# A filler step between logits and transposes, and row scales behind the next block, in a two-layer retention and differential-attention trunk

## The chip, the core and the metric

The kernel runs on one core of a Trainium2 chip. The metric is the device time of one execution in microseconds (us), taken as the median of several runs. Behind the times stands a profile of one execution: every instruction of the five engines with its start and duration, the DMA transfers, and the clock that was granted to TensorE. In the profile PE is TensorE, DVE is VectorE, ACT is ScalarE, POOL is GpSimd and SP is SyncE, which only issues DMAs.

## The reference

Two layers over 1024 tokens of width 1024, float32. Layer 0 is a retention mixer, layer 1 differential attention with 16 heads; each has an input projection with a SiLU gate, an output projection and RMS norms around it. The change lies in layer 1:

```python
def block(args):                       # 128 queries against all keys, per head
    qblk, start = args
    logits = jnp.einsum('bhmqd,bhmkd->bhmqk', qblk, k)    # m: two maps per head, d = 64
    logits = jnp.where(mask, logits + bias[None, :, None], -jnp.inf)
    probs = jax.nn.softmax(logits, axis=-1)
    attn = probs[:, :, 0] - lam * probs[:, :, 1]
    return jnp.einsum('bhqk,bhke->bhqe', attn, v)

out = lax.map(block, (qb, starts))
out = rmsnorm(out, subln_g, eps=GN_EPS) * (1.0 - lambda_init)   # per head and query
gated = jax.nn.silu(g) * out
return gated @ w_out
```

## The kernel before

Products are made at nearly float32 precision from pairs of fp32r parts, high and low: each product of two operands is three matmuls (high x high, high x low, low x high). Layer 1 is `attention_layer`. Its main loop runs over 16 heads and, in each, over 8 blocks of 128 queries in the order 6, 2, 3, 7, 4, 0, 1, 5 (`ORDER`); block i sees the keys of blocks 0 to i. One turn of the loop, a step, does this:

- `logits` of the next block (lines 760 to 767): full-width products for the high parts (L760), then narrow ones over 64 rows of the array for the low parts (L767), or, for blocks 0 and 1, products with a query padded with zeros (L763). They go to two PSUM tiles "S", one for each of the two maps.
- `attn_t` of the present block (L821): up to four transposes of the probabilities e, by TensorE, into the one PSUM bank "T"; ScalarE copies them out as `ath` (L824) and VectorE makes `atl` (L825). Blocks 4 to 7 have a second group of transposes later in the step.
- `softmax` of the next block, on VectorE and ScalarE: maxima (L792, L794), negation (L795), exponentials that read S (L797), then reciprocal and combination of the two maps into e (L800, L801, L803).
- `square_sum` of the last finished pair of blocks (L857, L858: products with ones), its copy `ssr` (L860) and a DMA to DRAM (`ssd`).
- after each odd block, `values` (L835 to L837) for a pair of blocks, with the squares (L843 to L845).

TensorE's order is written out by hand: instructions stand in it as the program issues them. The other engines' order is set by the scheduler of the framework. Between these pieces TensorE is given filler: a generator, `filler_gen`, that yields steps of three 512-wide products (lines 215 to 217, and 616 to 618 for the gates; or three 256-wide ones, 658 to 660), all projections of later heads, and at its end the first products of the output projection (lines 122 to 124 in `out_mm`). `pull` takes one step and adds its estimated cost to a clock `clk`; `fill_until(t)` pulls until that clock reaches t; `fill_total` keeps the supply at a steady pace at the end of each step. `ready` is the clock time from which the transposes of the next block may be issued; it is counted from the logits by `SLACK["base"]` and `SLACK["wide"]`. When the supply is empty `pull` does nothing.

Heads are gathered in three batches, 0 to 7, 8 to 11 and 12 to 15. At the end of a batch the square sum of its last pair is made at once, and in the next step `row_scales` loads all square sums of the batch (`rss`), transposes the softmax sums in bank "T" (L869), copies them to `rsr` (L872) and makes the row scales (L873, L874 and the reciprocal root). Pieces of the gated output are then scaled one per step by `finish`. The last batch's row scales come behind the loop.

Of the kernel before, what the change touches and what calls it, by code (L numbers as in the profile page):

```python
# [50 lines left out]
class _Trunk:  # L51
# [525 lines left out]
    def attention_layer(self, HR, QR, pmm, ws0, slots):  # L577
        nc, io = self.nc, self.io
        with ExitStack() as es:
# [308 lines left out]
            for _ in v_proj(0):  # L888
                pass
            pend = None  # L890
            rows = None
            todo = []
            ready = 0.0
            ready_o = 0.0
# [1 line left out]
            for s, (h, i) in enumerate(seq):  # L896
# [4 lines left out]
                if nxt is not None:  # L901
                    if nxt[0] not in bts:
                        load_bias(nxt[0])
                    need("qk", nxt[0])
                    if s % TB == 2:
                        narrow_q(h)
                    need("qk", seq[min(s + AHEAD, len(seq) - 1)][0])
                    fill_until(ready - SLACK["qk"])
                    Ss = logits(*nxt)
                    nready = clk["pe"] + SLACK["base"] + SLACK["wide"] * (nxt[1] + 1) / 8.0  # L910
                fill_until(ready)
                attn_t(h, i, A, 0)
                t_done = clk["pe"]
                if rows is not None:
                    row_scales(*rows)
                    todo += [None] * 8 + [(tb, h0) for h0 in range(*BATCHES[rows[0]], 4) for tb in range(TB)] + [()]
                    rows = None
                elif todo:
                    step = todo.pop(0)
                    if step:  # L920
                        finish(*step)
                    elif step == ():
                        finish_store()
# [7 lines left out]
                if pend is not None:  # L931
                    fill_until(ready_o)
                    square_sum(*pend)
                    pend = None
                if i % 2 == 1:
                    need("v", h // 2)
                    if h < LATE:
                        need("g", h)
                    fill_until(t_done + SLACK["av"])
                    pend = (h, i // 2) + values(h, i // 2)  # L940
                    ready_o = clk["pe"] + SLACK["sq"]
                    if i == ORDER[-1] and h + 1 in (BATCHES[0][1], BATCHES[1][1]):
                        fill_until(ready_o)
                        square_sum(*pend)
                        pend = None
                        rows = (batch(h)[0],)
                n_ = s + 1
                if RATE * n_ / 8.0 <= total:
                    fill_total(RATE * n_ / 8.0)
# [144 lines left out]
```

## Time and profile before

| | us |
|---|---|
| median of three runs | 2177.19 |
| lowest, highest | 2174.77, 2178.92 |
| the profiled execution | 2180.56 |
| span of its instructions | 2178.6 |
| attention loop in the span | about 922 to 2005 |

The profiled execution is 2 us longer than its span, from the first to the last instruction. Layer 0 fills the span up to 922 us, the attention loop follows, and from 2005 us the output projection of layer 1. In the timeline each row has the start in us from the span's start, the duration, the engine, the line, the operation, what is written and read, shapes and the number of instructions that are merged (x4), and in brackets the idle time of the engine ahead of it and what ended that. TensorE's instructions overlap: a 512-wide product lasts 0.4 us, but the next one starts 0.235 us behind it.

### The profile page before, as it was taken

How to read it: one execution, taken by the hardware profiler on the slowest of the kernel's cores; microseconds unless marked ns; L12 is line 12 of the kernel's file. 1: busy time of each engine (PE TensorE's matmuls, PEld its weight loads, DVE VectorE, ACT ScalarE, POOL GpSimd, SP SyncE). 2: the span in 40 equal slices, each digit the busy share in tenths (PEclk: the TensorE clock that was granted, in tenths of full speed). 3: DMA queues.
4: the chain of work that ended last, by engine and by line, in shares of the span. 5: the costliest groups of instructions: out<-in, count | busy, mean ns of one | idle time of the engine just before them, and what ended most of it. 6: DMA issues, size and time to landing. Idle time of an engine off the chain costs nothing.

```text
span 2178.6 us, 31078 instructions
## 1 busy us (share of the span) xinstructions
PE 2130.3 (98%) x11861; PEld 1793.9 (82%) x11861; DVE 1293.9 (59%) x3188; ACT 851.5 (39%) x1638; POOL 427.4 (20%) x246
## 2 busy tenths in 40 slices
PE   7999999999999999999999999999999999999998
PEld 7888988898897788787888888888787878877876
DVE  6254344434437438736777667777777777776644
ACT  4121221122123333335555455554545555544321
POOL 2332501511512000121111111111133111211300
PEclk9999999999999999999999999999999999999999
DMA  4112112111212544311111111111244113334743
GB/s 164 65 39 68 57 39 73 47 54 54 63 55 98 176 158 166 121 49 42 40 46 42 40 49 42 39 37 43 85 136 134 47 38 95 115 101 146 256 152 133
DMA packets 98916, 185.48 MB, mean 85 GB/s; under 512 B 8848, under 2 KB 51024, under 8 KB 98640
## 3 DMA queue, kind: packets, MB, share of 16 engines
q1 hardware_dynamic: 63824, 166.50, 23.5%
q10 hardware_dynamic: 34944, 17.01, 2.6%
q8 instruction: 93, 1.52, 0.3%
q14 instruction: 55, 0.45, 0.1%
HBM read 147.67 MB, written 38.95 MB: 86 GB/s over the span
## 4 chain that ended last, share of the span: by engine, by line
PE 89%; DVE 4%; DMA 3%; issue 2%; ACT 1%; SPq 0%; POOL 0%; DVEq 0%; ACTq 0%; POOLq 0%
PE ps_mm L158 6%; PE ps_mm L157 6%; PE ps_mm L159 5%; PE ps_mm L215 5%; PE ps_mm L216 5%; PE ps_mm L217 5%; PE ps_mm L122 4%; PE ps_mm L123 4%; PE ps_mm L124 4%; PE ps_t L821 3%; PE ps_ret L398 3%; PE ps_s L760 3%; PE ps_mm L658 3%; PE ps_mm L167 3%; PE ps_mm L169 3%; PE ps_mm L168 3%
## 5 line engine op out<-in xcount | busy, mean ns | idle before, releaser
L83 POOL TENSOR_TENSOR w_l<-w_raw,w_h 128x1024 fp32r<-128x1024 f32 x112 | 271.6, 2431 | 1169.3 <-ACT w_h L82 1137.6
L797 ACT ACTIVATE e<-ps_s,nm 128x896 f32<-128x896 f32 (+7 forms) x256 | 189.8, 742 | 111.3 <-DVE nm L795 101.9
L215 PE MATMUL ps_mm<-RB,w_h 128*128 128x512 f32 x512 | 209.8, 410 | 0.4 <-ACT RB L150 0.4
L157 PE MATMUL ps_mm<-RA,w_h 128*128 128x512 f32 x512 | 204.6, 400 | 1.2 <-DVE sg L428 1.1
L158 PE MATMUL ps_mm<-RA,w_h 128*128 128x512 f32 x512 | 205.4, 401 | 0.0
L216 PE MATMUL ps_mm<-RB,w_h 128*128 128x512 f32 x512 | 202.9, 396 | 1.5 <-DVE RB L151 1.5
L217 PE MATMUL ps_mm<-RB,w_l 128*128 128x512 f32 x512 | 202.7, 396 | 0.0
L159 PE MATMUL ps_mm<-RA,w_l 128*128 128x512 f32 x512 | 202.4, 396 | 0.0
L824 ACT CAST ath<-ps_t 128x512 fp32r<-128x512 f32 (+1 forms) x192 | 91.9, 478 | 221.4 <-PE ps_t L821 205.5
L82 ACT CAST w_h<-w_raw 128x1024 fp32r<-128x1024 f32 x112 | 117.5, 1049 | 123.5 <-PE ps_mm L158 38.8
L792 DVE TENSOR_REDUCE mx<-ps_s 128x1 f32<-128x640 f32 (+2 forms) x192 | 119.4, 622 | 76.7 <-PE ps_s L767 72.5
L111 DVE TENSOR_TENSOR g_l<-w_raw,g_h 128x1024 fp32r<-128x1024 f32 x60 | 84.1, 1402 | 107.4 <-ACT g_h L110 107.3
L658 PE MATMUL ps_mm<-w_h,RB 128*128 128x256 f32 x512 | 147.3, 288 | 0.0
L169 PE MATMUL ps_mm<-w_h,RA 128*128 128x256 f32 x512 | 145.6, 285 | 0.0
L167 PE MATMUL ps_mm<-w_h,RA 128*128 128x256 f32 x512 | 144.9, 285 | 0.6 <-ACT RA L150 0.6
L168 PE MATMUL ps_mm<-w_l,RA 128*128 128x256 f32 x512 | 144.8, 284 | 0.1
L660 PE MATMUL ps_mm<-w_h,RB 128*128 128x256 f32 x512 | 143.5, 280 | 0.0
L659 PE MATMUL ps_mm<-w_l,RB 128*128 128x256 f32 x512 | 143.5, 280 | 0.0
L110 ACT CAST g_h<-w_raw 128x1024 fp32r<-128x1024 f32 x60 | 62.9, 1049 | 167.9 <-PE ps_mm L123 125.5
L157 PEld LDWEIGHTS ps_mm<-RA,w_h 128*128 128x128 f32 x512 | 96.4, 188 | 24.7 <-DVE sg L428 1.6
L217 PEld LDWEIGHTS ps_mm<-RB,w_l 128*128 128x128 f32 x512 | 96.5, 189 | 23.7
L159 PEld LDWEIGHTS ps_mm<-RA,w_l 128*128 128x128 f32 x512 | 96.6, 189 | 22.4
(216 smaller groups left out, 5408.4 us busy)
## 6 DMA issues: line engine op xcount, KB each, us to landing
w_raw<-in_wn SPq DMA_DIRECT2D x64, 512.0 KB
w_raw<-in_wv SPq DMA_DIRECT2D x32, 512.0 KB
w_raw<-in_wo SPq DMA_DIRECT2D x32, 512.0 KB
w_raw<-g SPq DMA_DIRECT2D x32, 512.0 KB
w_raw<-g1f SPq DMA_DIRECT2D x24, 512.0 KB
xt<-in_x SPq DMA_DIRECT2D x16, 512.0 KB
w_raw<-in_wg SPq DMA_DIRECT2D x16, 512.0 KB
g<-go ACTq DMA_DIRECT2D x32, 256.0 KB
```

What stands on the lines that cost most here:

```text
L83: nc.gpsimd.tensor_sub(l, raw, _f32(h))
L157: nc.tensor.matmul(ps, wh[:, k], region[:, kt, cols], start=(kt == 0), stop=False)
L158: nc.tensor.matmul(ps, wh[:, k], region[:, 8 + kt, cols], start=False, stop=False)
L159: nc.tensor.matmul(ps, wl[:, k], region[:, kt, cols], start=False, stop=(kt == KT - 1))
L167: nc.tensor.matmul(ps, region[:, kt, cols], wh[:, k], start=(kt == 0), stop=False)
L168: nc.tensor.matmul(ps, region[:, kt, cols], wl[:, k], start=False, stop=False)
L169: nc.tensor.matmul(ps, region[:, 8 + kt, cols], wh[:, k], start=False, stop=(kt == KT - 1))
L215: nc.tensor.matmul(ps, wh[:, k], HR[:, kt, tok], start=(kt == 0), stop=False)
L216: nc.tensor.matmul(ps, wh[:, k], HR[:, 8 + kt, tok], start=False, stop=False)
L217: nc.tensor.matmul(ps, wl[:, k], HR[:, kt, tok], start=False, stop=(kt == KT - 1))
L658: nc.tensor.matmul(ps[:, t, :], HR[:, kt, cols], wh[:, k], start=(kt == 0), stop=False)
L797: nc.scalar.activation(e[:, 0:n], S[:, 0:n], AF.Exp, bias=nm, accum_out=(s0 if m == 0 else s1))
```

## The change

One filler step is pulled right behind the logits, and `ready` is counted from behind it. `row_scales` moves ahead of the transposes of its step. At the end of a batch the square sum is no longer made at once, but, as all others, in the following step, behind that step's transposes; the row scales then come one step later than before.

```diff
--- before.py
+++ after.py
@@ -888,7 +888,7 @@
             for _ in v_proj(0):
                 pass
             pend = None
-            rows = None
+            rows = closing = None
             todo = []
             ready = 0.0
             ready_o = 0.0
@@ -907,12 +907,14 @@
                     need("qk", seq[min(s + AHEAD, len(seq) - 1)][0])
                     fill_until(ready - SLACK["qk"])
                     Ss = logits(*nxt)
+                    pull()
                     nready = clk["pe"] + SLACK["base"] + SLACK["wide"] * (nxt[1] + 1) / 8.0
+                if rows is not None:
+                    row_scales(*rows)
                 fill_until(ready)
                 attn_t(h, i, A, 0)
                 t_done = clk["pe"]
                 if rows is not None:
-                    row_scales(*rows)
                     todo += [None] * 8 + [(tb, h0) for h0 in range(*BATCHES[rows[0]], 4) for tb in range(TB)] + [()]
                     rows = None
                 elif todo:
@@ -932,6 +934,8 @@
                     fill_until(ready_o)
                     square_sum(*pend)
                     pend = None
+                    if closing is not None:
+                        rows, closing = (closing,), None
                 if i % 2 == 1:
                     need("v", h // 2)
                     if h < LATE:
@@ -939,11 +943,8 @@
                     fill_until(t_done + SLACK["av"])
                     pend = (h, i // 2) + values(h, i // 2)
                     ready_o = clk["pe"] + SLACK["sq"]
-                    if i == ORDER[-1] and h + 1 in (BATCHES[0][1], BATCHES[1][1]):
-                        fill_until(ready_o)
-                        square_sum(*pend)
-                        pend = None
-                        rows = (batch(h)[0],)
+                    if i == ORDER[-1] and h + 1 in [h1 for h0, h1 in BATCHES[:-1]]:
+                        closing = batch(h)[0]
                 n_ = s + 1
                 if RATE * n_ / 8.0 <= total:
                     fill_total(RATE * n_ / 8.0)
```

How this moves instructions is seen on TensorE. In an ordinary step of head 0 (the logits of block 2 in L760 and L767, then the first transposes of block 6):

```order
 L760 MATMUL ps_s<-RA 128x384 x2
 L767 MATMUL ps_s<-RA 128x384 x2
+L215 MATMUL ps_mm<-RB,w_h 128x512
+L216 MATMUL ps_mm<-RB,w_h 128x512
+L217 MATMUL ps_mm<-RB,w_l 128x512
 L821 MATMUL ps_t<-ident,e 128x128 x4
 L215 MATMUL ps_mm<-RB,w_h 128x512
```

The three products of a filler step stand between the narrow products and the transposes; the same supply has one step less further on.

The end of the first batch on TensorE, before: the square sum of head 7 (L857, L858), the logits of head 8, the transposes of its first block, the row-scale transpose L869, and filler.

```order
L857 MATMUL ps_o<-sqh,ones 128x256
L858 MATMUL ps_o<-sql,ones 128x256
L760 MATMUL ps_s<-RA 128x384 x2
L767 MATMUL ps_s<-RA 128x384 x2
L821 MATMUL ps_t<-ident,e 128x128 x4
L869 MATMUL ps_t<-ident,s0all 64x128
L616 MATMUL ps_mm<-RB,w_h 128x512
L617 MATMUL ps_mm<-RB,w_h 128x512
```

Now: the end of the transposes of head 8's first block, the square sum of head 7, and, after four filler steps that are left out, the logits of the next block, one filler step, L869 and the transposes.

```order
L821 MATMUL ps_t<-ident,e 128x128 x3
L857 MATMUL ps_o<-sqh,ones 128x256
L858 MATMUL ps_o<-sql,ones 128x256
...
L760 MATMUL ps_s<-RA 128x512 x2
L767 MATMUL ps_s<-RA 128x512 x2
L616 MATMUL ps_mm<-RB,w_h 128x512
L617 MATMUL ps_mm<-RB,w_h 128x512
L618 MATMUL ps_mm<-RB,w_l 128x512
L869 MATMUL ps_t<-ident,s0all 64x128
L821 MATMUL ps_t<-ident,e 128x128 x3
L616 MATMUL ps_mm<-RB,w_h 128x512
```

L869 stands ahead of the transposes that use the same bank and one step later, and the square sum behind transposes.

The last block of the last head on TensorE, before: its logits (L760, L767), the transposes of the block ahead of it (x2), filler, its own transposes (x4, x2) and the square sum. The first gap holds eight more filler steps and six value products, the second two filler steps.

```order
L760 MATMUL ps_s<-RA 128x384 x4
L767 MATMUL ps_s<-RA 128x384 x4
L821 MATMUL ps_t<-ident,e 128x128 x2
L122 MATMUL ps_mm<-RA,g_h 128x512
L123 MATMUL ps_mm<-RA,g_h 128x512
L124 MATMUL ps_mm<-RA,g_l 128x512
...
L821 MATMUL ps_t<-ident,e 128x128 x4
...
L821 MATMUL ps_t<-ident,e 128x128 x2
L857 MATMUL ps_o<-sqh,ones 128x256
```

Behind these logits 11 filler steps stand ahead of the last transposes. Now:

```order
L760 MATMUL ps_s<-RA 128x384 x4
L767 MATMUL ps_s<-RA 128x384 x4
L821 MATMUL ps_t<-ident,e 128x128 x2
L835 MATMUL ps_o<-ath,RA 128x256
L836 MATMUL ps_o<-atl,RA 128x256
L837 MATMUL ps_o<-ath,RA 128x256
...
L821 MATMUL ps_t<-ident,e 128x128 x6
L857 MATMUL ps_o<-sqh,ones 128x256
L858 MATMUL ps_o<-sql,ones 128x256
L835 MATMUL ps_o<-ath,RA 128x256
```

No filler is left behind these logits; the six transposes stand in one row, and the gap holds value products only (L837 among them). On VectorE, in the same place, before: the combination of the block ahead (L803, 256 wide), then the first maximum of the last block, and the copy of the transposes.

```order
L803 SCALAR_TENSOR_TENSOR e<-e,arr 128x256
L792 TENSOR_REDUCE mx<-ps_s 128x1
L794 ISA ps_s,mx<-ps_s,bt,mx 128x256
L794 ISA mx 128x1
L825 TENSOR_TENSOR atl<-ps_t,ath 128x2x128
L795 TENSOR_SCALAR nm<-mx 128x1
```

The maximum follows the combination at once. Now the low part of a gated tile (L111, for the output projection) stands between them.

```order
L803 SCALAR_TENSOR_TENSOR e<-e,arr 128x256
L111 TENSOR_TENSOR g_l<-w_raw,g_h 128x1024
L792 TENSOR_REDUCE mx<-ps_s 128x1
L825 TENSOR_TENSOR atl<-ps_t,ath 128x2x128
L794 ISA ps_s,mx<-ps_s,bt,mx 128x256
```

L111 has moved ahead of the last block's first maximum; before it stood behind that block's second negation.

## Rows read from the trace of the kernel before

**Rows 1.** The page: its head, and part 1, busy time, share of the span and instructions.

```profile
span 2178.6 us, 31078 instructions
...
PE 2130.3 (98%) x11861; PEld 1793.9 (82%) x11861; DVE 1293.9 (59%) x3188; ACT 851.5 (39%) x1638; POOL 427.4 (20%) x246
```

**Rows 2.** Who waited for whom, TensorE, 922 to 1990 us: total, times, longest.

```profile
PE ps_t L821 <- DVE atl L825: 4.6, 4, 2.0
PE ps_t L821 <- DVE e L803: 4.0, 5, 1.8
PE ps_s L760 <- ACT e L797: 3.3, 3, 1.2
PE ps_t L869 <- DVE atl L825: 2.8, 2, 1.4
PE ps_o L836 <- DVE atl L825: 2.3, 1, 2.3
PE ps_o L836 <- DVE nm L795: 1.9, 3, 0.8
```

**Rows 3.** Timeline of TensorE (start, us, work), a block's transposes right behind narrow products.

```profile
1240.28 0.73 PE L767 MATMUL ps_s<-RA 64*128 64x512 f32 x4
1240.94 0.66 PE L821 MATMUL ps_t<-ident,e 128*128 128x128 f32 x4
```

**Rows 4.** Timeline of TensorE, a filler step right behind narrow products.

```profile
1693.15 0.50 PE L215 MATMUL ps_mm<-RB,w_h 128*128 128x512 f32 x1
1693.48 0.40 PE L216 MATMUL ps_mm<-RB,w_h 128*128 128x512 f32 x1
1693.72 0.39 PE L217 MATMUL ps_mm<-RB,w_l 128*128 128x512 f32 x1
```

**Rows 5.** Timeline of TensorE, transposes behind a filler, and behind padded-query products.

```profile
1970.79 0.60 PE L821 MATMUL ps_t<-ident,e 128*128 128x128 f32 x4
...
1976.80 0.62 PE L821 MATMUL ps_t<-ident,e 128*128 128x128 f32 x4
```

**Rows 6.** Timeline of TensorE, the longest wait for the probabilities.

```profile
1641.76 0.63 PE L821 MATMUL ps_t<-ident,e 128*128 128x128 f32 x4 [1.83 <-DVE e L803]
```

**Rows 7.** Timeline of all engines, end of the first batch of heads; idle time in brackets.

```profile
1487.80 0.30 PE L869 MATMUL ps_t<-ident,s0all 128*64 128x128 f32 x1 [1.40 <-DVE atl L825]
...
1491.41 0.28 DVE L874 SCALAR_TENSOR_TENSOR rsv<-rss,rsv 64x128 f32<-64x128 f32 x1 [2.43 <-DMA rss<-ssd]
...
1494.24 0.55 PE L821 MATMUL ps_t<-ident,e 128*128 128x128 f32 x3 [0.73 <-DVE atl L825]
```

**Rows 8.** Timeline of all engines, the last head's last block.

```profile
1989.37 0.61 PE L767 MATMUL ps_s<-RA 64*128 64x384 f32 x4
...
1993.69 1.23 DVE L111 TENSOR_TENSOR g_l<-w_raw,g_h 128x1024 fp32r<-128x1024 f32 x1 [0.55 <-ACT g_h L110]
...
1995.88 1.02 DVE L803 SCALAR_TENSOR_TENSOR e<-e,arr 128x768 f32<-128x768 f32 x1
...
1997.18 0.60 PE L821 MATMUL ps_t<-ident,e 128*128 128x128 f32 x4
...
1998.43 0.69 DVE L825 TENSOR_TENSOR atl<-ps_t,ath 128x512 fp32r<-128x512 f32 x1 [1.54 <-ACT ath L824]
...
1999.18 0.44 PE L821 MATMUL ps_t<-ident,e 128*128 128x128 f32 x2
```

**Rows 9.** Groups by line, TensorE, 1990 to 1999.1 us.

```profile
L122 PE MATMUL ps_mm<-RB,g_h 128*128 128x512 f32 x8 | 3.3, 411 | 0.0
...
L122 PE MATMUL ps_mm<-RA,g_h 128*128 128x512 f32 x3 | 1.3, 426 | 0.0
```

**Rows 10.** Timeline of TensorE, first wait behind the attention stage.

```profile
2075.73 0.50 PE L124 MATMUL ps_mm<-RB,gl 128*128 128x512 f32 x1 [0.98 <-DVE gl L477]
```

**Rows 11.** Sums by stretch: us, busy time of PE, PEld, DVE, ACT, POOL, then PEclk.

```profile
1927.80:1931.20 3.40, 3.40 (x11) 2.89 (x11) 2.06 (x7) 2.24 (x5) 0.00 (x0) 0.50 0.84 297
1982.40:1985.80 3.40, 2.94 (x12) 2.15 (x12) 2.85 (x9) 0.59 (x2) 0.00 (x0) 0.50 0.39 142
```

## Prediction

> **What bounds the kernel now.** I read the page first: TensorE is busy for 2130.3 of 2178.6 us [rows 1]. Nothing else comes near, so only three things can move the time: TensorE's idle time, the pace of its instructions, and its clock. The change touches the attention loop alone (about 922 to 2005 us of the span). The list of TensorE's waits in that stretch, up to 1990 us, is therefore the whole purse: 19 us in all [rows 2], of which 4.0 us are transposes that wait for the finished row of probabilities (L821 behind L803), 4.6 us transposes and 2.3 us value products that wait for VectorE's copy of an earlier transpose (L825), 3.3 us logits whose PSUM is still read by the exponentials (L797), and 2.8 us the two row-scale transposes (L869). Over the stage's 1083 us that is under 2%, so a small loss elsewhere can eat any gain. What follows attention moves one for one with its end: the first product there that waits for data, at 2075.73, still stands 0.98 us behind a transfer chain that starts at the last square sum [rows 10].
>
> **The change, part by part.** Work is conserved: the filler steps (three products, 0.70 us at 0.235 us from start to start [rows 4]) are a fixed supply, and each one pulled behind the logits is one fewer elsewhere.
>
> *One filler between logits and transposes, price on TensorE.* Today the transposes follow the narrow products (L767, 64 rows of the array) at once [rows 3]: four of them then take 0.66 us, against 0.60 us when they follow a full-width filler [rows 5]. When a filler follows the narrow products, its second product starts 0.33 us after its first, where 0.24 us is usual [rows 4]. So the moved switch costs about 0.10 us and gives back 0.06 us: +0.04 us a block. The instruction order has 90 such blocks with the transposes directly behind; 1 is left, so 89 x 0.04 = +3.6 us. Behind the 16 one-block logits (query padded with zeros) the transposes take 0.62 us [rows 5] and only gain 0.02 us: -0.3 us. Together **+3.3 us**; ends 0 (the switch costs the same wherever it falls) and +5.
>
> *The waits for L803.* A block's transposes now come at least one filler (0.70 us) later after their own logits, and two (1.40 us) where the due time decides, because that time is counted from after the pull. The longest wait is 1.83 us [rows 6]; the other four, 2.2 us together, are under 0.8 us each. With two fillers 0.4 us is left, with one 1.2 us: **-3.4 us**, ends -2.8 and -4.0.
>
> *Batch ends.* The filler in front of the square sum and the square sum itself only change places with other work: nothing. The row-scale transpose used to wait 1.40 us, right behind the block's transposes, for the one bank "T" [rows 7]. Now it goes first and finds the bank free, but the block's transposes right behind it wait for VectorE's copy of it (L872), which stands in VectorE's queue behind the next block's maximum. The nearest row is the wait that it replaces, 1.40 us; the one filler ahead covers up to 0.70 us of it. I take half of that cover at each of two places: -0.7 us. Also, the square sum is now a step ahead of the row scales, so that L874's wait for the loaded sums (2.43 us, all of VectorE behind it) shrinks and with it the transposes' wait of 0.73 us at 1494.24 [rows 7]: -0.7 us. **-1.4 us**, ends 0 and -3.5.
>
> *The end of the last head.* This term decides. Pulling earlier empties the supply earlier. Before, between the last block's logits (they end at 1989.98) and its transposes at 1997.18 and 1999.18 [rows 8] there lie 11 filler steps [rows 9], 11 x 0.70 = 7.7 us: they are the work that hides the last softmax, and its e is ready only at 1996.90, 7 us after the logits. In the changed order not one filler stands there: logits, two transposes, six value products, then the six transposes. All 11 have been spent earlier, where TensorE was busy anyway and they lengthen the way to these logits by 7.7 us, while the stretch from the logits to the end cannot shrink: it is the softmax chain (0.3 us of slack only), then the copy out of "T" before the last two transposes (done at 1999.12, so the 2 us between the two groups stay). Hence **+7.7 us**. In VectorE's new order the 1.23 us subtraction L111 stands ahead of the chain's first step instead of beside the exponentials [rows 8]: +0.4 us, ends -1.6 (nothing on VectorE in its way) and +1.2.
>
> *The clock.* Stretches of 3.4 us at half speed (0.50, which is 1.2 GHz) stand in the trace at 1927.8 and 1982.4 [rows 11], each just behind one of the two longest waits, 2.3 and 2.0 us [rows 2]. The new idle at the end, some 5 us in one piece, should bring another; a half-speed stretch full of products costs 1.7 us, and here half of it is waiting: **+0.8 us**, ends 0 and +3.4.
>
> *All other waits*, 12 us in rows 2 (L825, L797, L795). Their slack is not changed by the rules (turn, av, sq stay), but the order of VectorE's queue around them is made anew. I take **-1.0 us**, ends -8 and +4.
>
> Sum: 3.3 - 3.4 - 1.4 + 7.7 + 0.4 + 0.8 - 1.0 = **+6.4 us**. The profiled execution took 2180.56 us, so its like would take 2187.0; the median of the three runs is 2177.19, 0.15% below that, and my number is for a median: **2183.6 us**.
>
> TensorEngine Tiling (Array Packing) in the Trainium skill, section Key Properties, says that changing the tiling mode drains TensorE. By it alone the switch back from 64 rows costs the same whatever comes next, and the first term would be 0. Rows 3 to 5 show two prices, 0.06 and 0.10 us, so I keep the term and make the rule a rival.
>
> **The rivals.** (1) *The switch is free to move*: 0 instead of +3.3, so +3.1 us, 2180.3. For it: a switch takes place once a block in either order. Against it: the two prices in rows 3 to 5, though the second comes from few places. It is the rule cited above. 10%. (2) *Half of the other waits go too*: transposes that come 0.70 us later find their copy L825 sooner in VectorE's order, since it stands behind the next block's first maximum there. Then -6 instead of -1: +1.4 us, 2178.6. For it: the waits are single accidents, 0.5 to 2.3 us, no pattern. Against it: each accident needs VectorE free, and its work is the same. 25%. (3) *Faster*: the same mechanism at full size, at L825 and L797. Where VectorE's queue was late by under 1.4 us at nearly all places, the shift clears it, and 16.5 us of the 19.4 must go before the result is 4.4 us ahead; with all but 2 us gone, and no further half-speed stretch, it is 3.3 + 8.1 - 17.4 = -6 us, 2171.2. Against it: the two longest (2.3 and 2.0 us) are longer than any shift the change makes. 9%. That the pull does nothing is no case but in the blocks that had a filler there already (6 of 96).
>
> **How the numbers follow.** Runs of this kernel spread over 0.2% (4 us), so less than 4.4 us is no change. The forecast, 56%, is slower by 4.4 to 13 us. Rivals 1 and 2 are within the bound, 35%; rival 3 is faster, 9%. The forecast's own range is 2181.5 to 2190; with rivals 1 and 2, and a piece of the unknown waits, 2175.5 to 2190 leaves some 2 in 10 outside. The sums of all the ends (-8 and +17 us) are not reached together.
>
> **What would show it.** Right: in the changed profile the six last transposes wait 5 us and more for L803 and then 1 to 2 us for L825; no filler lies between them and the last logits; the waits of L821 for L803 elsewhere fall from 4.0 to about 0.6 us; products L215 and L616 behind L767 start their second 0.33 us after the first, some 90 times; L869 has no wait and the transposes behind it about 1 us each. Wrong: if the last logits start at the old time although 11 fillers moved ahead of them, more waits went than I allow; if the attention waits other than the tail's grow by over 4 us, VectorE's new order, not the tail, is the cost.

## The result, and the profile after

The changed kernel takes **2196.49 us** (median of four runs, 2193.69 to 2197.96) where the kernel before took 2176.66 on the same chip (2174.77 to 2178.92). The ratio on record is 1.0082, 95% interval 1.0070 to 1.0093: slower, by 18 us by the ratio and by 19.8 us by the two medians. Forecast were 2183.6 us, 6.4 us slower, with a range up to 2190.0. The sign was right; the size was about three times too small.

The profiled execution of the changed kernel took 2197.28 us, 16.7 more than that of before. The head of its page and part 1 (busy time, share of the span, instructions):

```profile
span 2195.2 us, 31124 instructions
...
PE 2138.9 (97%) x11861; PEld 1794.2 (82%) x11861; DVE 1295.8 (59%) x3188; ACT 847.7 (39%) x1638; POOL 430.7 (20%) x246
```

TensorE runs the same 11861 matmuls [rows 1], yet is busy 8.6 us longer, and the span grew by 16.6. So half of the loss is not idle time at all. To see where it lies I added up, over TensorE's instructions in each trace, the attention stage from its first logits to the first product behind it. "Body" is idle time up to the last logits, "tail" idle time behind them, "half speed" is the busy time in stretches with a granted clock of 0.50; "pace" is what is left of the stage when the idle time and half of the half-speed time (what it costs, if work there takes twice as long) are taken off.

| profiled execution | stage | body | tail | half speed | pace |
|---|---|---|---|---|---|
| before | 1063.9 | 19.7 | 2.3 | 6.4 | 1038.7 |
| changed | 1081.7 | 19.9 | 9.6 | 9.7 | 1047.3 |

The stage accounts for +17.8 us: +0.2 in the body's waits, +7.3 in the tail, +1.6 for the clock, +8.6 in pace. (With -3.4 us ahead of the stage and +2.2 behind it this makes the 16.6 of the span. Ahead of the stage, where the change alters nothing, the run of before has two stretches of 3.4 us at a granted clock of 0.50, at 709.2 and 917.4, and the changed one has none; at half pace that makes the 3.4 us.)

**The body.** Who waited for whom on TensorE, 922 to 1990 us: total, times, longest.

```profile
PE ps_o L836 <- DVE atl L825: 7.6, 6, 2.3
PE ps_t L821 <- DVE nm L795: 5.6, 6, 1.5
PE ps_t L821 <- DVE atl L825: 4.4, 4, 1.4
PE ps_s L760 <- ACT e L797: 1.3, 2, 0.7
PE ps_t L821 <- DVE e L803: 0.7, 2, 0.4
```

Against [rows 2], L869's waits are gone, the logits' wait for L797 fell from 3.3 to 1.3, and by name L821 waits only 0.7 us for L803 (4.0 before). But the value products' wait for L825 rose from 2.3 to 7.6, and the transposes' row with L795 from 0.5 to 5.6; it was, before:

```profile
PE ps_t L821 <- DVE nm L795: 0.5, 1, 0.5
```

The name L795 misleads. Timeline, VectorE and TensorE around one of these waits:

```profile
1168.07 0.61 DVE L803 SCALAR_TENSOR_TENSOR e<-e,arr 128x384 f32<-128x384 f32 x1
1168.60 0.15 DVE L795 TENSOR_SCALAR nm<-mx 128x1 f32<-128x1 f32 x1
1168.83 0.41 PE L821 MATMUL ps_t<-ident,e 128*128 128x128 f32 x2 [1.17 <-DVE nm L795]
```

L803, which makes the operand, ended at 1168.68; L795, which the transposes don't read, ended after it and got the name. Put down to the instruction that makes the operand or frees the bank, L803 still costs 3.5 us (4.3 before, read in the same way), and the value products' wait for L825 rose from 4.2 to 7.7 us, since [rows 2] has 1.9 us of it under L795 too. All waits for L825, of value products and of transposes behind transposes, rose from 9.3 to 13.8 us.

**The tail.** Timeline of the last head's last block:

```profile
2000.93 0.62 PE L767 MATMUL ps_s<-RA 64*128 64x384 f32 x4
2001.18 1.22 DVE L111 TENSOR_TENSOR g_l<-w_raw,g_h 128x1024 fp32r<-128x1024 f32 x1 [0.28 <-ACT g_h L110]
...
2007.79 1.02 DVE L803 SCALAR_TENSOR_TENSOR e<-e,arr 128x768 f32<-128x768 f32 x1
2008.95 1.09 PE L821 MATMUL ps_t<-ident,e 128*128 128x128 f32 x4 [4.77 <-DVE e L803]
...
2011.44 0.69 PE L821 MATMUL ps_t<-ident,e 128*128 128x128 f32 x2 [1.40 <-DVE atl L825]
```

In [rows 8] neither group waited: 11 filler steps [rows 9] stood in front. Now the first waits 4.77 us for the last softmax and the second 1.40 us for the copy of the first.

**The clock.** Sums by stretch (us, busy time of PE, PEld, DVE, ACT, POOL, then PEclk):

```profile
1774.70:1778.10 3.40, 3.40 (x14) 2.92 (x13) 2.03 (x5) 1.88 (x4) 0.00 (x0) 0.50 0.05 17
2006.80:2017.00 10.20, 6.05 (x26) 5.42 (x26) 2.83 (x6) 1.46 (x4) 0.00 (x0) 0.50 0.04 13
```

With the wait of 4.77 us came 10.2 us at half speed (1.2 GHz) in one piece, where before such stretches were 3.4 us long [rows 11].

**The pace, and the origin of the new waits.** Timeline of one step of the body, a pulled filler between narrow products and transposes:

```profile
1812.39 0.68 PE L767 MATMUL ps_s<-RA 64*128 64x448 f32 x4
...
1813.00 0.49 PE L215 MATMUL ps_mm<-RB,w_h 128*128 128x512 f32 x1
...
1813.33 0.40 PE L216 MATMUL ps_mm<-RB,w_h 128*128 128x512 f32 x1
...
1813.57 0.39 PE L217 MATMUL ps_mm<-RB,w_l 128*128 128x512 f32 x1
...
1813.80 0.60 PE L821 MATMUL ps_t<-ident,e 128*128 128x128 f32 x4
1813.81 1.05 ACT L82 CAST w_h<-w_raw 128x1024 fp32r<-128x1024 f32 x1 [4.21 <-PE ps_mm L216]
...
1814.77 0.59 ACT L222 ACTIVATE RA<-ps_mm 64x512 fp32r<-64x512 f32 x1
...
1815.36 0.60 ACT L223 ACTIVATE RA<-ps_mm 64x512 fp32r<-64x512 f32 x1
...
1815.98 0.59 ACT L824 CAST ath<-ps_t 128x512 fp32r<-128x512 f32 x1
...
1816.24 0.68 DVE L224 SCALAR_TENSOR_TENSOR RA<-ps_mm,RA 64x512 fp32r<-64x512 f32 x1
...
1816.94 0.69 DVE L225 SCALAR_TENSOR_TENSOR RA<-ps_mm,RA 64x512 fp32r<-64x512 f32 x1
...
1817.85 0.69 DVE L825 TENSOR_TENSOR atl<-ps_t,ath 128x512 fp32r<-128x512 f32 x1
...
1818.60 0.44 PE L821 MATMUL ps_t<-ident,e 128*128 128x128 f32 x2 [1.40 <-DVE atl L825]
```

Two things are to be seen. L216 starts 0.33 us behind L215: the switch back from 64 rows. And the pulled step was the last on its PSUM bank. It freed a weight tile, so ScalarE first rounds the next weight (L82, 1.05 us), then copies the filled bank out (L222, L223; such copies of a filler's bank are called its evacuation below); only then comes the copy of the transposes, L824, 1.58 us after they ended (1814.40). On VectorE the bank's low parts (L224, L225) stand ahead of L825. TensorE needs the bank "T" again at 1817.2 and waits.

A step that ends a bank is called a closing step below. Counted in TensorE's order, 5 of the 192 transpose groups stood directly behind one; now 14 do. Counted in the trace, 25 of 189 copies L824 in the body had an evacuation between them and their transposes; now 34 of 189. From the transposes' end to the end of L825 it takes 1.5 us on the mean without an evacuation, 2.6 us with one. Counted in waits: of the 9.3 us for L825 before, 0.7 stood behind a copy with an evacuation in front; of the 13.8 us now, 11.5 do (4.5 of them also behind a VectorE instruction that took 1.2 to 2.0 us more than its like beside GpSimd, on which more below).

### The profile page after: what moved, and what is told of

Same layout as the page of the kernel before. It is cut to its first block, busy times and chain, and to the rows that moved or that the text cites. A ratio compares the mean times of both kernels' runs of the same rounds, so it can differ in the third digit from the quotient of the medians.

```text
span 2195.2 us, 31124 instructions
## 1 busy us (share of the span) xinstructions
PE 2138.9 (97%) x11861; PEld 1794.2 (82%) x11861; DVE 1295.8 (59%) x3188; ACT 847.7 (39%) x1638; POOL 430.7 (20%) x246
## 4 chain that ended last, share of the span: by engine, by line
PE 85%; DVE 5%; DMA 5%; issue 2%; POOL 1%; ACT 1%; SPq 0%; DVEq 0%; POOLq 0%; ACTq 0%
PE ps_mm L158 5%; PE ps_mm L157 5%; PE ps_mm L159 5%; PE ps_mm L215 5%; PE ps_mm L216 5%; PE ps_mm L217 5%; PE ps_mm L124 4%; PE ps_mm L122 4%; PE ps_mm L123 4%; PE ps_ret L398 3%; PE ps_mm L167 3%; PE ps_mm L168 3%; PE ps_mm L169 3%; PE ps_s L760 3%; PE ps_mm L658 2%; PE ps_t L821 2%
## 5 line engine op out<-in xcount | busy, mean ns | idle before, releaser
L797 ACT ACTIVATE e<-ps_s,nm 128x896 f32<-128x896 f32 (+7 forms) x256 | 190.2, 744 | 79.8 <-DVE nm L795 76.4
L215 PE MATMUL ps_mm<-RB,w_h 128*128 128x512 f32 x512 | 214.7, 419 | 0.4 <-ACT RB L150 0.4
L216 PE MATMUL ps_mm<-RB,w_h 128*128 128x512 f32 x512 | 202.7, 396 | 1.5 <-DVE RB L151 1.5
L217 PE MATMUL ps_mm<-RB,w_l 128*128 128x512 f32 x512 | 202.5, 395 | 0.0
L824 ACT CAST ath<-ps_t 128x512 fp32r<-128x512 f32 (+1 forms) x192 | 91.9, 479 | 211.5 <-PE ps_t L821 189.3
L82 ACT CAST w_h<-w_raw 128x1024 fp32r<-128x1024 f32 x112 | 117.6, 1050 | 142.7 <-issue 39.9
L792 DVE TENSOR_REDUCE mx<-ps_s 128x1 f32<-128x640 f32 (+2 forms) x192 | 119.4, 622 | 81.8 <-PE ps_s L767 75.1
L111 DVE TENSOR_TENSOR g_l<-w_raw,g_h 128x1024 fp32r<-128x1024 f32 x60 | 82.7, 1378 | 106.5 <-ACT g_h L110 106.4
L215 PEld LDWEIGHTS ps_mm<-RB,w_h 128*128 128x128 f32 x512 | 96.6, 189 | 29.2 <-issue 12.9
L217 PEld LDWEIGHTS ps_mm<-RB,w_l 128*128 128x128 f32 x512 | 96.5, 188 | 23.5
```

The lines of the kernel that those rows point to most:

```text
L215: nc.tensor.matmul(ps, wh[:, k], HR[:, kt, tok], start=(kt == 0), stop=False)
L216: nc.tensor.matmul(ps, wh[:, k], HR[:, 8 + kt, tok], start=False, stop=False)
L217: nc.tensor.matmul(ps, wl[:, k], HR[:, kt, tok], start=False, stop=(kt == KT - 1))
L797: nc.scalar.activation(e[:, 0:n], S[:, 0:n], AF.Exp, bias=nm, accum_out=(s0 if m == 0 else s1))
```

## The experiments

All ratios are to the kernel before, run beside it on the same chip; the changed kernel stands at 1.0082. The times of a row are those of its one profiled execution. 0.001 is 2.2 us. Line numbers of edited kernels are shifted by a few lines where rows are shown.

| run | ratio, 95% interval | stage | body | tail | half speed | pace |
|---|---|---|---|---|---|---|
| pull alone | 1.0127 (1.0114 to 1.0140) | 1091.4 | 25.9 | 9.6 | 17.6 | 1047.2 |
| rows alone | 1.0000 (0.9992 to 1.0008) | 1065.3 | 18.1 | 2.3 | 12.4 | 1038.7 |
| due time ahead of the pull | 1.0079 (1.0067 to 1.0091) | 1081.1 | 22.7 | 4.6 | 12.4 | 1047.6 |
| no pull in the last 16 | 1.0055 (1.0044 to 1.0066) | 1079.8 | 23.9 | 2.3 | 16.3 | 1045.4 |
| filler ahead of narrow | 1.0050 (1.0037 to 1.0063) | 1075.5 | 21.0 | 9.6 | 8.5 | 1040.6 |
| no closing step ahead | 1.0055 (1.0043 to 1.0067) | 1077.1 | 15.8 | 9.4 | 14.1 | 1044.8 |
| the three together | 1.0006 (0.9997 to 1.0015) | 1065.0 | 20.0 | 2.3 | 6.9 | 1039.2 |
| changed, low parts in four | 1.0075 (1.0062 to 1.0088) | 1083.1 | 20.5 | 9.8 | 14.1 | 1045.7 |
| before, low parts in four | 0.9972 (0.9961 to 0.9984) | 1059.0 | 14.8 | 2.3 | 6.9 | 1038.5 |
| rows, low parts in four | 0.9965 (0.9951 to 0.9978) | 1055.6 | 12.5 | 2.3 | 3.3 | 1039.2 |
| rows, low parts in four, no closing step | 1.0005 (0.9997 to 1.0014) | 1063.9 | 18.0 | 2.3 | 8.5 | 1039.3 |
| rows, low parts in four, output weights too | **0.9938** (0.9924 to 0.9951) | 1051.3 | 9.0 | 2.7 | 0.0 | 1039.5 |

### The two halves of the change alone

Pull alone: the changed kernel with the batch ends as before.

```diff
-                if rows is not None:
-                    row_scales(*rows)
                 fill_until(ready)
                 attn_t(h, i, A, 0)
                 t_done = clk["pe"]
                 if rows is not None:
+                    row_scales(*rows)
...
-                    if i == ORDER[-1] and h + 1 in [h1 for h0, h1 in BATCHES[:-1]]:
-                        closing = batch(h)[0]
+                    if i == ORDER[-1] and h + 1 in (BATCHES[0][1], BATCHES[1][1]):
+                        fill_until(ready_o)
+                        square_sum(*pend)
+                        pend = None
+                        rows = (batch(h)[0],)
```

> Only the filler behind the logits; square sums and row scales as in the kernel before. If the row-scale part gained the 1.4 us of the prediction (it removed 2.8 us of waits at L869 and brought 1.3 us in front of the transposes behind it), this kernel takes about 2198, 1.4 us more than the changed one (2196.5). Rival: the row-scale part is itself a loss, through the new order of VectorE's queue around it; then this kernel takes 2194 or less.

Rows alone: the changed kernel without the line `pull()` behind the logits.

> Only the square sum and the row scales moved behind the next block's work; no filler behind the logits. TensorE's order then differs from the kernel before at two places only. Theory: 1.4 to 2.8 us less than the kernel before (2176.7), so 2174 to 2175.3. Rival: the two moved row scales cost as much as they save, 2177 to 2179.

The row-scale part alone is no change that can be measured: its trace has 1.6 us less idle time in the body, as expected, but 6 us more at half speed, which costs 3. The pull alone is 28 us slower, 10 us worse than with the other part; neither theory expected that much. Tail and pace are those of the changed kernel; the difference is in the body (25.9 against 19.9 us) and the clock. The largest single piece, timeline of all engines:

```profile
1803.77 1.05 ACT L82 CAST w_h<-w_raw 128x1024 fp32r<-128x1024 f32 x1 [1.32 <-issue]
...
1804.72 0.57 ACT L228 CAST RA<-ps_mm 64x512 fp32r<-64x512 f32 x1
...
1804.90 2.35 POOL L83 TENSOR_TENSOR w_l<-w_raw,w_h 128x1024 fp32r<-128x1024 f32 x1 [14.95 <-ACT w_h L82]
...
1805.00 2.39 DVE L593 CAST qz<-RA 64x256 fp32r<-64x256 f32 x1
...
1805.91 0.27 ACT L824 CAST ath<-ps_t 128x128 fp32r<-128x128 f32 x1
...
1809.70 0.29 DVE L825 TENSOR_TENSOR atl<-ps_t,ath 128x128 fp32r<-128x128 f32 x1
...
1810.14 0.45 PE L821 MATMUL ps_t<-ident,e 128*128 128x128 f32 x1 [4.70 <-DVE nm L795]
```

Again a weight's rounding and an evacuation ahead of L824; and on VectorE a small copy (L593) that takes 2.39 us beside a GpSimd subtraction of 2.35. The loss belongs to the pull. How much the body adds on top differs with the order around it, here mostly by this one wait; why the row-scale part is worth 10 us beside the pull and nothing alone is not shown beyond that.

### The tail

Due time ahead of the pull:

```diff
-                    pull()
                     nready = clk["pe"] + SLACK["base"] + SLACK["wide"] * (nxt[1] + 1) / 8.0
+                    pull()
```

> The changed kernel with one line lower: the due time of the transposes is counted from before the pulled step, not after it. The pull then brings the transposes one filler step later at most instead of two, and six filler steps are left between the last logits and the last transposes (none in the changed kernel, 11 in the one before). The tail theory (idle time of 7 us because the supply is spent) expects 6 x 0.70 = 4.2 us of it back: 2192. If in addition the body's waits for VectorE's copies come from the second step of delay, they fall too, from 20 us to 14 or less, and the time is 2187. Rival: the loss is the pace behind the switch from 64 rows alone, which stays the same for every block: 2196.

The tail gave back 5.0 us, as the tail theory has it, but the time is the rival's. Not for the rival's reason, though: the body lost 2.8 us and the clock 1.3. With the due time a step earlier, 30 transpose groups stand directly behind a closing step, where the changed kernel has 14, and 43 copies have an evacuation in front, where it has 34.

No pull in the last 16 steps:

```diff
-                    pull()
+                    if s < 112:
+                        pull()
```

> The changed kernel, but without the filler behind the logits in the last 16 of the 128 steps. Only 11 of the 127 pulled fillers go; the tail then has its 11 fillers between the last logits and the last transposes again, as in the kernel before. Tail theory: the 7.3 us of new idle time there go, and with them the half-speed stretch behind it (some 3 us): 9 to 10 us less than the changed kernel, a ratio to before of 1.0038. Rival: the time was only moved, and the last 16 steps lose as much in other waits, as in the run with the due time lower: ratio 1.007 or more.

With 11 of the 127 pulled fillers left out the tail is 2.3 us again and the kernel 5.9 us faster (0.0027). That is less than the 9 to 10 expected (the profiled execution, 2196.05 us, was the longest of the six, whose median is 2192.08). The body's old waits in these steps came back with the old order (2.18 us at 1998.99, as 1.95 us in the kernel before): 4 us more in the body than in the changed kernel. So the spent supply costs the whole 7.3 us of idle time in the tail, and the pulls in the last two heads had bought some of it back in waits.

### The switch from 64 rows

```diff
+                if i >= 2 and clk["go"]:
+                    pull()
                 if i < 2:
                     for m in range(2):
                         nc.tensor.matmul(Ss[m][:, cuts[0]], qz[:, 256 * m + i * P:256 * m + (i + 1) * P], kl(h)[:, cuts[0]], start=False, stop=True)
...
-                    pull()
+                    if nxt[1] < 2:
+                        pull()
```

> The changed kernel, but where the logits end with narrow products (64 rows of the array) the filler step stands between the full-width products L760 and the narrow ones, so that the transposes follow the narrow products directly again, as before. The tail is as in the changed kernel (no filler left). Switch theory, by the pace of the trace (some 8 us of the 10 us more of TensorE's time without idle time): about 8 us less than the changed kernel, 2188. By the term of the prediction (0.04 us a block, 95 blocks): 3.8 us less, 2193. Rival, the switch costs the same wherever it falls: 2196.

7 us less (0.0032), and by the trace 6.7 us less in pace, with the tail unchanged. Timeline of TensorE in this kernel, filler (L215 to L217), narrow products (here L769), transposes (here L823):

```profile
1806.48 0.39 PE L215 MATMUL ps_mm<-RB,w_h 128*128 128x512 f32 x1
1806.71 0.39 PE L216 MATMUL ps_mm<-RB,w_h 128*128 128x512 f32 x1
1806.95 0.40 PE L217 MATMUL ps_mm<-RB,w_l 128*128 128x512 f32 x1
1807.27 0.68 PE L769 MATMUL ps_s<-RA 64*128 64x448 f32 x4
1807.88 0.66 PE L823 MATMUL ps_t<-ident,e 128*128 128x128 f32 x4
```

L216 starts 0.23 us behind L215 again, and the four transposes pay the switch with 0.66 us, as in [rows 3]. The rule of the Trainium skill that the prediction made a rival (TensorEngine Tiling (Array Packing), Key Properties: a change of the tiling mode drains TensorE) says nothing of what stands behind the switch; these runs show that its price depends on it.

### Evacuations ahead of the transposes' copies

The closing `yield` of a bank is marked by its value, and `clk["n"]` counts the steps since:

```diff
-                    pull()
+                    if clk["n"] != clk["last"]:
+                        pull()
...
-                fill_until(ready)
+                if fill_until(ready) and clk["n"] == 0:
+                    pull()
```

> The changed kernel, but no filler step that closes a PSUM bank is put directly ahead of a block's first transposes (the pull is left out where the next step closes a bank, and where the due time pulls a closing step, one more follows). Queue theory: the bank's evacuation then no longer stands ahead of the transposes' copies on ScalarE and VectorE. Copies with an evacuation between the transposes' end and L824 fall from 34 of 190 to 20 or fewer, those that also stand behind a weight's rounding (L82) from 6 to 2 or fewer, the body's waits from 20 to 13 us, and the time to 7 us less than the changed kernel (ratio 1.005). Rival: the waits are accidents of the order, and a new order brings as many: ratio 1.008, body's waits 18 us or more.

5.9 us less than the changed kernel. Groups directly behind a closing step fell from 14 to 3, copies with an evacuation in front from 34 to 26 (20 or fewer were expected; those behind L82 too, from 6 to 3), the waits for L825 behind such copies from 11.5 to 4.1 us, the body's waits from 19.9 to 15.8 us: the direction of the queue theory, at some six tenths of its size in the waits. Of the stage's 4.6 us all waits make 4.3 and the pace 2.5 (15 more blocks have no pull, so no moved switch); the clock takes 2.2 back.

### All three together

The three edits in one kernel (the pulled step ahead of the narrow products by the same rule, and not in the last 16 steps).

> The changed kernel with the three edits of the runs before together: the filler stands ahead of the narrow products instead of behind them, none is put there where the next step closes a bank (and a closing step that the due time pulls is followed by one more), and none in the last 16 steps. If the switch (7 us in its run), the copies behind evacuations (6 us) and the spent supply (6 us) are three separate costs that add up, 19 of the 18 to 20 us go: ratio 0.999 to 1.001, attention's idle time 18 us or less. Rival: the three runs gained from one common thing, such as fewer pulled steps; then the ratio stays at 1.003 or more.

7.0, 5.9 and 5.9 us are 18.8 us; together 16.6 us went, down to no measurable difference from before. But that the sum comes out is partly luck. In the trace the 16.7 us of the stage are pace (8.1), tail (7.3) and clock (1.4); the body, which the evacuation rule alone had lowered by 4.1, is 20.0 us. So the switch and the spent supply are two separate costs; that the evacuations are a third that adds to them is not shown by this run. Waits for L825 behind an evacuation are 2.3 us here (11.5 in the changed kernel), but those for L803 are 7.0 (3.5), and in the last two heads the waits of the kernel before are back. The gain that the pull was to bring in the body's waits is not there in this kernel either, though the filler is pulled at most of the first 112 steps.

### GpSimd beside VectorE

In the kernel before, two rows of the timeline just ahead of its longest wait [rows 6]:

```profile
1638.13 2.39 POOL L83 TENSOR_TENSOR w_l<-w_raw,w_h 128x1024 fp32r<-128x1024 f32 x1
...
1638.60 3.02 DVE L803 SCALAR_TENSOR_TENSOR e<-e,arr 128x1024 f32<-128x1024 f32 x1
```

L803 takes 1.28 us at this size elsewhere. So, from the attention loop on, in `load_w` (and likewise in `load_out`, where the low parts that VectorE makes are cut too):

```diff
-        nc.gpsimd.tensor_sub(l, raw, _f32(h))
+        n = 1024 // getattr(self, "cut", 1)
+        for c in range(0, 1024, n):
+            nc.gpsimd.tensor_sub(l[:, c:c + n], raw[:, c:c + n], _f32(h[:, c:c + n]))
```

> The kernel before, with GpSimd's subtractions of a weight's low part (L83, L94) cut into four pieces of 256 columns in the attention stage. In the trace of before, all 14 VectorE instructions that took over 0.4 us more than their like ran beside a GpSimd instruction, and ended with it; three of the longest waits (1.83, 2.32 and 1.95 us) stand behind such a one. If GpSimd holds VectorE for one instruction at a time, a piece of 0.6 us holds it for a quarter, and the kernel takes 4 to 6 us less than before: ratio 0.998. Rival: the pieces follow each other so closely that VectorE is held through all four, or the order is made anew with as many waits: ratio 1.0.

> The changed kernel, with GpSimd's subtractions cut into four pieces in the same way. It has 19 such held VectorE instructions (14 before), and the waits at 1458.24 and 1939.70 us stand behind two of them. If held VectorE instructions explain why the body's waits did not fall, this one gains more than the cut gives the kernel before, 6 to 8 us: ratio 1.005. Rival: the waits are evacuations ahead of the transposes' copies and the cut gives about as much as it gives before: ratio 1.006 to 1.008.

The kernel before gained 6.1 us (0.9972), the changed one 1.5 (1.0075, an interval that contains 1.0082). The same place in the cut kernel (L807 is L803 there, L825 is L821):

```profile
1635.80 2.41 POOL L85 TENSOR_TENSOR w_l<-w_raw,w_h 128x256 fp32r<-128x256 f32 x2
...
1636.17 1.45 DVE L807 SCALAR_TENSOR_TENSOR e<-e,arr 128x1024 f32<-128x1024 f32 x1
...
1637.77 0.30 PE L825 MATMUL ps_t<-ident,e 128*128 128x128 f32 x1 [0.55 <-DVE e L807]
```

The hold is 0.2 us instead of 1.7, the wait 0.55 instead of 1.83. Of the three waits that the expectation named it is the only one that fell: the other two places have 2.31 and 2.17 us, the first with three pieces that VectorE makes itself ahead of the copy, the second with L111 (L115 there). The rest of the 4.9 us that the body lost is mostly two waits of 1.19 us for L797, at 1730.25 and 1765.37, which stood behind other held instructions (L593, L72, L74) and are gone. For the changed kernel the rival holds: of its two named waits that at 1458.24 fell from 2.29 to 0.64 us, that at 1939.70 stayed (2.49), others came, and 10.0 us of waits behind evacuations are left of 11.5.

### Versions faster than both

> The kernel before with the row-scale part of the change and with GpSimd's subtractions in four pieces; no filler behind the logits. The cut alone gave a ratio of 0.9972. The row-scale part should take off the two waits of 1.40 us at L869 and the 1.06 us behind them and bring about 1.3 us: ratio 0.9964. Rival: as in its run alone, where its 1.6 us of idle time did not show: 0.9972 or a little more.

> The same, and a filler step that closes a bank is never the last ahead of transposes (either group): one more is pulled behind it. Copies L824 with an evacuation between them and their transposes stand at 25 of 190 in the kernel before; 15 or fewer are left, and the waits of 0.7 to 1.2 us behind such copies go: ratio 0.995. Rival: the extra step only moves the evacuation behind the transposes' own copy of the next group, and the time stays where the kernel without this edit is.

The row-scale part on top of the cut gives 0.9965, which the intervals don't tell from 0.9972. The rule for closing steps in both transpose groups, put into this kernel, is a loss of 9 us: no group stands directly behind a closing step any more, but 27 copies still have an evacuation in front (25 before), and the new order brought a wait of 3.47 us behind one of them. A step of 0.7 us is shorter than the rounding (1.05) and the evacuation (1.2), so a longer distance, or the closing step behind the transposes, may do better; no run tried it here.

In the 0.9965 kernel the longest wait of the body is this (timeline; L98 is L94, L829 is L825, L840 is L836):

```profile
1914.99 2.47 DVE L98 TENSOR_TENSOR RA<-w_raw,RA 128x256 fp32r<-128x256 f32 x3
1917.38 0.68 DVE L796 TENSOR_REDUCE mx<-ps_s 128x1 f32<-128x512 f32 x1
1917.98 0.41 DVE L829 TENSOR_TENSOR atl<-ps_t,ath 128x256 fp32r<-128x256 f32 x1
...
1918.45 0.39 PE L840 MATMUL ps_o<-atl,RA 128*128 128x256 f32 x1 [2.31 <-DVE atl L829]
```

The last edit takes L98 off VectorE in the stage (four of the eight low parts made there were on it, not two of four):

```diff
-        eng = nc.vector if (t % 2 == 0) else nc.gpsimd
+        eng = nc.vector if (t % 2 == 0 and (layer, hf) != (1, 0)) else nc.gpsimd
```

> As the run with the row-scale part and the four pieces, and the low parts of the output weights that are loaded during attention (two of four were on VectorE) are all made on GpSimd in pieces. In that run's trace the longest wait left, 2.31 us at 1918.45, stands behind three such VectorE pieces of 0.73 to 0.96 us ahead of the transposes' copy. If they cause it, the wait falls to 0.5 us or less and the time by 2 to 4 us with the half-speed stretch that follows such a wait: ratio 0.995. Rival: the next thing in VectorE's queue takes their place: 0.9965.

2165.6 us (2164.68 to 2167.13), ratio 0.9938: 13 us faster than the kernel before and more than was expected. The named wait fell from 2.31 to 0.10 us; a second one, of 2.23 us at 1971.97 in the 0.9965 kernel, is gone too, which was not aimed at. The body's waits are 9.0 us, and the stage has no stretch at half speed (the next one starts as it ends, at 1990.1). Its longest waits, TensorE, 922 to 1990 us:

```profile
PE ps_t L825 <- DVE e L807: 3.2, 6, 0.8
PE ps_o L840 <- DVE nm L799: 1.9, 3, 0.8
PE ps_t L825 <- DVE rsr L876: 1.6, 2, 1.1
```

None over 1.1 us is left in the body.

## Why the prediction was wrong, point by point

**The tail: right.** Forecast were +7.7 and +0.4 us; the tail's idle time rose by 7.3. The signs came nearly as stated: no filler behind the last logits, 4.77 us for L803 (5 and more were stated) and then 1.40 us for L825. The run without the last 16 pulls shows it alone.

**The price of the switch: mechanism right, size too small.** The term was +3.3 us, its end +5. In the changed trace the second product behind narrow ones starts 0.339 us after the first at 75 places and 0.226 us at 19 (256 columns), where 0.234 and 0.118 are usual, so +0.105 us; the transposes give back 0.053. That is +0.05 us in 94 blocks, 4.9 us; the padded blocks, forecast at -0.3, add 0.5, because a filler pays behind them too. The pace as a whole rose by 8.6 us, past my end, and 6.7 of it went when the filler was put ahead of the narrow products. The 3 us between 5.4 and 8.6 I can only partly place: about 1 us are restarts behind the added waits, and where the other 2 us lie stays open. In the run with the three edits 8.1 of the 8.6 are gone.

**The waits for L803 (-3.4) and all other waits (-1.0): here the prediction failed.** It reasoned that transposes which come one or two fillers later find their operand ready, and took the rest of VectorE's order as noise of either sign. The body's waits did not shrink: 19.7 to 19.9 us. The old waits went as it said, and further: at none of the seven places where L803 was waited for before is it waited for now, and the waits for L825 without an evacuation ahead of the copy fell from 8.6 to 2.3 us. New ones took their place: L803 costs 3.5 us (4.3 before) at five other places, and the waits behind an evacuation are 11.5 us (0.7 before), so that the waits other than L803's and L869's rose by 2.5 us. A pulled step is not neutral time. It moves the ends of PSUM banks, and every eighth step (every sixteenth of V) releases an evacuation, for a bank of the queries 1.2 us on ScalarE and 1.4 us on VectorE, often behind 1.05 us of weight rounding. Ahead of the transposes, that work goes in front of their copies. The prediction counted the pulled step's three products and none of the instructions that it releases on the other engines. The run that keeps closing steps away from the transposes took 7.4 of the 11.5 us away, so that part is shown. What makes L803 late at its new places is not: evacuations stand in those chains, but in those of before as well. And the run with the three edits, with 2.3 us behind evacuations and 7.0 for L803, shows that even then the body's waits don't fall.

**The batch ends (-1.4): right in the trace, too small to matter.** L869 finds its bank free, and the transposes behind it wait less than the "about 1 us each" of the signs:

```profile
1498.83 0.27 PE L869 MATMUL ps_t<-ident,s0all 128*64 128x128 f32 x1
...
1499.81 0.44 PE L821 MATMUL ps_t<-ident,e 128*128 128x128 f32 x2 [0.71 <-DVE nm L795]
```

There and 0.57 us at the other batch end, so -1.5 us with the 2.8 us of [rows 2] gone. L874's wait for the loaded sums is gone at these places too, and with it the transposes' 0.73 us of [rows 7], which are counted with the other waits here. In the run of this part alone it does not show in the time.

**The clock (+0.8): right in sign, partly by luck.** 3.3 us more at half speed, 1.6 us: the 10.2 us at the tail's wait came, as forecast, but of the body's three waits of 2.2 to 2.3 us only one, at 1773.96, was followed by such a stretch, where both of the long ones before were [rows 11].

Sum of what was measured in the stage: 8.6 - 0.8 - 1.5 + 7.3 + 1.6 + 2.5 = +17.7 us; forecast +6.4. Of the 11 us between them 5.3 are the pace and 6.1 the waits of the body that stayed (2.6 of L803, 3.5 of the others). The rivals all lay on the other side, with fewer waits still. The stated test "if the waits other than the tail's grow by over 4 us, VectorE's new order is the cost" did not fire, since they grew by 0.2: it looked for a rise and should have asked whether the expected fall came.

## What to carry to other kernels

A step that is moved brings all that it releases: ask of each moved filler whether it ends a bank or frees a buffer, and what then enters the queues of ScalarE and VectorE ahead of a copy that TensorE waits for. A fixed supply of filler that is used earlier is missing where nothing else hides a chain, so look first at its end. And before moving work between waits, look at what the long ones have in common: here several stood behind one long instruction on GpSimd or VectorE, and cutting such instructions and moving four of them to the other engine gave, with the row-scale part, 13 us, where filler and row scales moved together lost 18.

## What the runs showed of the hardware that was not expected

**Some VectorE instructions are held by GpSimd for a whole instruction.** All 14 VectorE instructions in the attention stage of before that took over 0.4 us more than their like, and all 19 in the changed kernel, ran beside a GpSimd instruction, and ended about their own usual time, or less, after it ended (not together with it, as the expectation has it). They read two operands from SBUF (L72, L74, L94, L801, L803, L845) or copy from SBUF to SBUF (L593, L594). Others were not held: in the trace of before 142 VectorE instructions started inside a GpSimd one that ran on for over 0.4 us more than they need, all of them reading PSUM or at most one small operand (L792, L794, L795, L825 and others), and none took over 0.4 us more than its like. With the subtractions in pieces, mostly of 0.7 to 0.9 us, the most that one lost was 1.1 us, beside an instruction that had not been cut (L741, 1.29 us); in the kernel before it was 2.2 us. The Trainium skill (SBUF — State Buffer, section SBUF: two separate sides) calls the port pair that VectorE and GpSimd share an exclusive lock, held for the whole instruction. The traces agree, with these numbers.

**The price of leaving 64-row products depends on what follows.** The second of two 128x512 products starts 0.105 us late, the second of four transposes 0.053 us.

**Long waits can be paid for twice.** A single wait of about 2 us was followed by 3.4 us at a granted clock of 0.50 in some places (1927.60 and 1982.17 before, 1773.96 in the changed kernel) and not in others: behind the changed kernel's waits of 2.29 us at 1458.24 and 2.19 us at 1939.70 the granted clock stayed at 1.00. The tail's 4.77 us, with 1.40 and 0.60 us close behind, came with 10.2 us at 0.50. In the fastest kernel, with no wait over 1.1 us in the body, the stage has no such stretch.
